# A three-layer network on one core: eight groups of four feature tiles as Strassen products

## The chip, the cores and the metric

The kernel runs on one NeuronCore of a Trainium2 chip. The metric is the device time of one launch in microseconds, median of several runs. 128-row tiles lie in on-chip memory (SBUF), matrix products accumulate in eight PSUM banks of 128x512 fp32. Five engines work side by side: TensorE (PE; PEld is its weight load), VectorE (DVE), ScalarE (ACT), GpSimd (POOL) and SyncE (SP), which issues most of the DMAs.

## What is computed

The reference takes `x` (512 tokens, 1024 features, fp32) through three layers: (a) a block with gated linear attention (GLA), dilated windowed attention, sigmoid gates over both, an MLP and an embedding gate; (b) an mLSTM with stick-breaking attention; (c) a multi-scale pooling layer. Only the start of the first layer matters here:

```python
h = rmsnorm(x, ln1[i])
hq, hk, hv, hr, ha, hatt, hgate = _split_cols(h @ w_in[i], SPLIT_SIZES)
# hatt: q, k, v of 3 groups x 4 heads x 128;  hq, hk, hv, hr: GLA;  hgate: two gates of 1024
g_gla, g_att = jnp.split(hgate, 2, axis=-1)
mix = (jax.nn.sigmoid(g_gla) * y_gla + jax.nn.sigmoid(g_att) * y_att) @ w_out[i]
```

So `h @ w_in` is a 512x1024 by 1024x9744 product in fp32 accuracy, whose columns feed attention, GLA and gates.

## The kernel before, in words

**Layout and accuracy.** Activations lie feature-major: eight tiles of 128 features by 512 tokens. Each fp32 operand is split into a rounded high part and a rest (`split`, L169: a copy on ScalarE into type fp32r, then a subtraction on VectorE). A product is three matmuls: high-high, high-low, low-high (`mm3`, L450; `mm`, L163).

**Chunks and units.** All weights are one stream, `wstream`, of 314 chunks of 128x1024 fp32 (512 KB), in the order of use. A unit of the program consumes one chunk. `fm` (L331) makes one output tile of 128 features by 512 tokens: 8 k-blocks by 3 matmuls of 512 columns, 24 in all. `tok` (L412) makes token-major tiles over several units. `fm(..., halves)` does the columns in two halves of 256, in a few places of layers two and three. PSUM gives four banks ("mm") to units and four ("q") to everything else.

**Order.** `run` (L285) walks the list of units. Before a unit it calls `split_chunk` (L214), which splits chunks up to three units ahead into one of four pairs of buffers (HL_BUFS) and issues DMAs of raw chunks (RAW_BUFS = 3). It then calls `pump` (L273), which advances up to two side generators (attention L878, GLA L1002) by a step when enough slots (units) have passed (LAG, L63) and PSUM banks are free, and takes one entry of `self.jobs`. Then it emits the unit's matmuls and its evacuation. The compiler orders each engine's queue once, before the run: an instruction earlier in this program order goes first, but one that is ready may overtake one that is not. On the chip every queue is then worked off in its order. All other tiles of 128x512 are taken from three pools of slots, 44, 16 and 16 (L51, `S` L96).

**Layer one.** `prologue` (L557) loads `xT` into `self.xt` and splits `ln1 * x`, not yet divided by the root mean square, into `xs` (16 tiles). `norm1` (L581) makes the factor per token, `r1`, in both layouts. Every evacuation of the layer then multiplies by it: `qk_unit` (L596) on VectorE (with a stride of four tokens for groups 1 and 2, "z order"), `v_units` (L610) on ScalarE, the gates (L674) by a multiplication on VectorE and a sigmoid on ScalarE. The units run thus: 6 q/k tiles of attention head 0, 12 of the three v products, then 18 q/k tiles of heads 1 to 3 (`qk_head1`, L625), each head followed by the start of its attention; the unit for GLA's decay (`narrow`, L356), 8 for GLA's v, then for each of four GLA heads q, k and two `sr` tiles; 8 gate tiles, a wait for all generators, and `yg`, `ya` (L685, L692) with the last 8 gate tiles between them.

## Time and profile before

| | us |
|---|---|
| median of 3 runs (range) | 1927.49 (1927.16 to 1927.97) |
| the profiled execution's own time | 1926.77 |
| its span, first to last instruction | 1925.1 |
| TensorE busy | 1902.5 |
| VectorE, ScalarE, GpSimd busy | 1090.1, 873.3, 93.7 |
| mean granted TensorE clock | 0.995 |
| HBM traffic | 178.55 MB read, 6.12 MB written, 96 GB/s |

The profile is of one execution; times in it count from its first instruction. Matmuls are pipelined: a matmul's own duration holds its way through the array, so the rate is read from a run of many of them, not from the duration of one. "Idle before" is the time for which the engine had nothing to do just before such an instruction, with what ended most of it. Instructions are named by the line of the helper that records them, so groups are told apart by shape and stretch. The profile finds a unit's end in the start of the ScalarE copy of the chunk four further on, which waits for that unit's buffer: by it 121.4 to 235 us holds the 18 q/k units of heads 1 to 3, 296.4 to 470 us the GLA heads and the first eight gates, 470 to 586 us `yg`, `ya` and the other eight gates.

### The profile page before, as it was taken

The numbers are of one execution on the slowest core, as the hardware profiler recorded it, in microseconds if no ns is written. First come the engines' busy times: TensorE is split into PE (matmuls) and PEld (weight loads), VectorE is DVE, ScalarE is ACT, GpSimd is POOL, SyncE is SP. The second block draws the span as 40 slices with busy tenths as digits, with TensorE's granted clock in tenths as the row PEclk, the third lists the DMA queues.
The fourth block names the chain that finished last, engine by engine and source line by source line (L and its number), as shares of the span: only waits on it lengthen the run. The fifth ranks groups of instructions, "written<-read, shape, count | busy, mean of one in ns | idle before, by whom it ended". The sixth has DMA issues, their size and how long they took to land.

```text
span 1925.1 us, 22678 instructions
## 1 busy us (share of the span) xinstructions
PE 1902.5 (99%) x8894; PEld 1598.1 (83%) x8894; DVE 1090.1 (57%) x1623; ACT 873.3 (45%) x1274; POOL 93.7 (5%) x125
## 2 busy tenths in 40 slices
PE   8999999999999999999998999999999999999998
PEld 7898888888888888888887888888888888888887
DVE  5245544577446543444556768677866627666733
ACT  4243344464223431333356666767666534433322
POOL 0000000000002000000120000011100011000000
PEclk9999999999999999999999999999999999999999
DMA  5442322222342322322232322222222322222222
GB/s 183 125 102 85 92 78 88 77 66 88 99 142 88 107 91 99 112 99 99 93 113 79 122 76 96 69 88 77 88 88 69 129 99 68 97 91 96 99 98 77
DMA packets 68095, 184.32 MB, mean 96 GB/s; under 512 B 17058, under 2 KB 20815, under 8 KB 67988
## 3 DMA queue, kind: packets, MB, share of 16 engines
q1 hardware_dynamic: 67412, 181.82, 29.3%
q8 instruction: 70, 1.15, 0.2%
q10 hardware_dynamic: 576, 1.05, 0.1%
q14 instruction: 37, 0.30, 0.0%
HBM read 178.55 MB, written 6.12 MB: 96 GB/s over the span
## 4 chain that ended last, share of the span: by engine, by line
PE 95%; DVE 3%; ACT 1%; issue 0%; DMA 0%; SPq 0%; POOL 0%; DVEq 0%; ACTq 0%; POOLq 0%
PE t L163 94%; DVE t L142 2%; ACT t L125 1%; DVE t L154 1%; PE t L973 0%; DMA t<-wstream 0%; PE t L1536 0%; ACT L125 0%; POOL t L500 0%; PE t L1045 0%; SPq L536 0%; ACT L136 0%; DVE t L1260 0%; SPq L533 0%; DVEq L1626 0%
## 5 line engine op out<-in xcount | busy, mean ns | idle before, releaser
L163 PE MATMUL t<-t,t 128*128 128x512 f32 (+3 forms) x8532 | 1862.2, 380 | 15.2 <-ACT t L125 9.4
L163 PEld LDWEIGHTS t<-t,t 128*128 128x128 f32 x8532 | 1549.9, 192 | 313.2 <-ACT t L125 12.7
L142 DVE TENSOR_TENSOR t<-t,t 128x1024 fp32r<-128x1024 f32 (+9 forms) x982 | 772.7, 815 | 718.4 <-ACT t L125 404.8
L125 ACT ACTIVATE t<-t 128x1024 fp32r<-128x1024 f32 (+6 forms) x883 | 633.8, 758 | 916.3 <-PE t L163 559.6
L154 DVE SCALAR_TENSOR_TENSOR t<-t,ct,t 128x512 f32<-128x512 f32 (+5 forms) x128 | 102.5, 815 | 15.4 <-ACT t L125 12.2
L154 DVE SCALAR_TENSOR_TENSOR t<-t,t 128x512 f32<-128x512 f32 (+6 forms) x112 | 76.4, 701 | 55.7 <-PE t L163 46.0
L125 ACT ACT_TABLE_LOAD x69 | 88.5, 1283 | 11.2 <-DVE t L154 8.6
L500 POOL TENSOR_TENSOR t<-t,t 128x512 f32<-128x512 f32 x33 | 52.2, 1588 | 577.0 <-ACT t L125 576.7
L125 ACT ACTIVATE t<-t,t 128x128 f32<-128x128 f32 (+4 forms) x93 | 50.3, 546 | 61.4 <-PE t L163 35.1
L125 ACT ACTIVATE t<-t,ct 128x512 f32<-128x512 f32 (+5 forms) x89 | 54.7, 624 | 19.9 <-DVE t L142 12.4
L197 POOL TENSOR_SCALAR_AFFINE_SELECT t<-t 128x128 f32<-128x128 f32 x80 | 36.4, 469 | 418.3 <-ACT t L125 222.4
L142 DVE TENSOR_TENSOR t<-t 128x511 f32<-128x511 f32 (+5 forms) x64 | 37.3, 586 | 1.2
L474 DVE RECIPROCAL t<-t 128x512 f32<-128x512 f32 (+3 forms) x15 | 28.1, 1870 | 13.6 <-ACT t L125 13.5
L154 DVE SCALAR_TENSOR_TENSOR t<-t,t,t 128x512 fp32r<-128x512 f32 (+3 forms) x41 | 27.6, 682 | 12.9 <-ACT t L125 12.7
L163 PE MATMUL t<-t,ct 128*128 128x256 f32 (+4 forms) x142 | 28.4, 335 | 0.0
L163 PEld LDWEIGHTS t<-t,ct 128*128 128x128 f32 (+1 forms) x142 | 21.5, 185 | 3.5 <-issue 1.0
L163 PEld LDWEIGHTS t<-ct,t 128*128 128x128 f32 x112 | 16.7, 220 | 0.7
L131 ACT ACTIVATE t<-t 128x512 f32<-128x512 f32 (+2 forms) x25 | 12.4, 561 | 10.3 <-PE t L163 7.7
L133 ACT ACT_TABLE_LOAD x13 | 16.7, 1283 | 0.2
L163 PE MATMUL t<-ct,t 128*128 128x1 f32 (+1 forms) x112 | 16.3, 278 | 0.0
L136 ACT ACTIVATE t<-t 128x512 f32<-128x512 f32 (+2 forms) x29 | 15.8, 594 | 0.2
L1517 ACT ACTIVATE t<-t 128x512 f32<-128x512 f32 x8 | 4.8, 598 | 23.7 <-PE t L163 23.7
(54 smaller groups left out, 133.0 us busy)
## 6 DMA issues: line engine op xcount, KB each, us to landing
t<-wstream SPq DMA_DIRECT2D x314, 512.0 KB, 3.3
t<-xT SPq DMA_DIRECT2D x16, 256.0 KB, 5.8
xdram<-t SPq DMA_DIRECT2D x8, 256.0 KB
t<-udram SPq DMA_DIRECT2D x8, 256.0 KB
t<-xdram SPq DMA_DIRECT2D x8, 256.0 KB, 5.5
out<-t ACTq DMA_DIRECT2D x4, 256.0 KB, 2.0
out<-t SPq DMA_DIRECT2D x4, 256.0 KB
skew<-bdram SPq DMA_DIRECT2D x2, 510.0 KB
```

The source lines that it names most:

```text
L125: self.pinned(self.nc.scalar.activation(out, in_, func, **kw))
L131: last = self.nc.scalar.activation(o, x, AF.Abs, bias=bias)
L133: last = self.nc.scalar.preload_act_table_set(EXPLN)
L136: last = self.nc.scalar.activation(o, o, AF.Exp, scale=-1.0)
L142: self.pinned(self.nc.vector.tensor_tensor(out, a, b, op=op))
L154: self.pinned(self.nc.vector.scalar_tensor_tensor(out, a, s, b, op0=op0, op1=op1))
L163: self.nc.tensor.matmul(out, lhsT, rhs, start=start, stop=stop, skip_group_check=True)
L197: self.nc.gpsimd.affine_select(t[:, 0:n], t[:, 0:n], pattern=[[1, n]], compare_op=op, fill=0.0, base=base, channel_multiplier=-1)
L474: self.nc.vector.reciprocal(out, out)
L500: self.nc.gpsimd.tensor_tensor(st[key], st[key], sq, op=ALU.add)
L1517: last = nc.scalar.activation(sq, ps, AF.Square, accum_out=ss[j][:, c:c + 1])
```

## The change

**Seven products for eight.** `quad` takes four feature tiles as two pairs. Each pair is a product of 256 features by 1024 by 512 tokens, seen as 2x2 blocks: two feature tiles, two halves of the features of `h`, two halves of the tokens. It is done in seven block products (Strassen's scheme in Winograd's form), each of 4 k-blocks by 3 matmuls of 256 columns. The seven units of a quad do the same product for both pairs, 24 matmuls of 256 columns each. Their weights come from four chunks, as before ("11", "12", "21", "22"); `third` makes the four sums of weight blocks on VectorE, and each of the seven blocks is split. The accumulators of a pair are two banks; the common partial sums are read out between the products (`snap`, ScalarE), and `c1` and `c2` put the output tiles together on VectorE and ScalarE. **Which groups:** 16 of the 18 q/k tiles of heads 1 to 3 (four quads), the q, k and `sr` tiles of GLA heads 0 and 1 (two) and the last eight gate tiles (two).

**Early normalisation.** Four jobs after `norm1` (`renorm`) multiply `xt` in place by `ln1` and `r1`, split the result into `xn` and build the sums of activation blocks (`forms`, `xf`). All units from the second v product on read `xn` or `xf`, and evacuate without `r1`, on ScalarE alone where VectorE multiplied before. `xs` ends after the first v product.

**Buffers.** One pool of 70 slots takes the place of 44, 16 and 16; RAW_BUFS goes from 3 to 6, of which three stay spare (one after the first layer's v products); `make` lets a unit take no chunk or two.

```diff
--- before.py
+++ after.py
 
-SLOTS = {'e': 44, 's': 16, 'r': 16}
-KIND = {"attention": "s", "gla": "r", "stick": "s", "mlstm": "r", "ml_out": "r", "ml_gates": "r"}
+SLOTS = 70
 TAIL = 2
...
+RAW_BUFS, HL_BUFS = 6, 4
+FAST_GLA, FAST_GATES = (0, 1), (4, 6)
 BIASW = (383, 255, 255)
 N_ONEHOT = sum(BIASW)
 
...
+
+    def raw_tile(self):
+        self.live += 1
+        return self.sb.tile([P, 1024], F32, name=self._nm(), tag="raw", bufs=RAW_BUFS)
+
+    def load_chunks(self, n=0):
+        while self.nd < self.nchunks and (self.nd < n or n == 0 and self.live < RAW_BUFS - self.spare):
...
             self.nc.sync.dma_start(t, self.io["wstream"][self.nd])
             self.raw[self.nd] = t
             self.nd += 1
 
+    def next_raw(self):
+        self.load_chunks(self.nr + 1)
+        self.nr += 1
+        return self.raw.pop(self.nr - 1)
+
+    def split_raw(self, raw):
+        h = self.sb.tile([P, 1024], F32R, name=self._nm(), tag="wh", bufs=HL_BUFS)
+        l = self.sb.tile([P, 1024], F32R, name=self._nm(), tag="wl", bufs=HL_BUFS)
+        self.act(h, raw, AF.Copy)
+        self.sub(l, raw, h.bitcast(F32))
+        return h, l
...
-            self.load_chunk(self.ns)
-            raw = self.raw.pop(self.ns)
-            h = self.sb.tile([P, 1024], F32R, name=self._nm(), tag="wh", bufs=HL_BUFS)
-            l = self.sb.tile([P, 1024], F32R, name=self._nm(), tag="wl", bufs=HL_BUFS)
-            self.act(h, raw, AF.Copy)
-            self.sub(l, raw, h.bitcast(F32))
-            self.hl[self.ns] = (h, l)
+            make = self.units[self.ns]["make"]
+            if make is None:
+                self.hl[self.ns] = self.split_raw(self.next_raw())
+                self.live -= 1
+            else:
+                self.hl[self.ns] = make()
             self.ns += 1
-            self.load_chunk(self.ns - 1 + RAW_BUFS)
+            self.load_chunks()
 
...
             return out
 
-        def both(out, r):
+        def both(out, r=None):
             n = out.shape[0]
+            if r is None:
+                self.act(out, st["ps"][0:n, :], AF.Copy)
+                self.add(out, st["ps"][64:64 + n, :], out)
+                return
...
+    def quad(self, specs, xf):
+        pairs = specs[0:2], specs[2:4]
+        st = [{} for _ in pairs]
+        r = {}
+
+        def take(*names):
+            for n in names:
+                r[n] = self.next_raw()
+
+        def done(n):
+            self.live -= 1
+            return self.split_raw(r.pop(n))
+
+        def first():
+            take("11")
+            return self.split_raw(r["11"])
+
+        def second():
+            take("12")
+            return self.split_raw(r["12"])
+
+        def third():
+            take("21", "22")
+            r["s1"] = self.raw_tile()
+            self.add(r["s1"], r["21"], r["22"])
+            self.sub(r["21"], r["11"], r["21"])
+            self.sub(r["11"], r["s1"], r["11"])
+            self.sub(r["12"], r["12"], r["11"])
+            return done("11")
+
+        makes = [first, second, third, lambda: done("s1"), lambda: done("21"), lambda: done("12"),
+                 lambda: done("22")]
+        L, R = HALVES
+
+        def order(t, z, sl=None):
+            if not z:
+                return t if sl is None else t[:, sl]
+            t = t.rearrange("p (z i) -> p z i", z=4)
+            return t if sl is None else t[:, :, sl.start // 4:sl.stop // 4]
+
+        def src(t, z):
+            return zs(t) if z else t
+
+        def compact(t, z):
+            return t.rearrange("p (z i) -> p z i", z=4) if z else t
+
+        def snap(p, bank, half, key, to, z, scale):
+            d = st[p]
+            if key not in d:
+                d[key] = self.S()
+            o = order(d[key], z, to) if key == "c1" else compact(d[key][:, to], z)
+            self.act(o, src(d[bank][:, half], z), AF.Copy, scale=scale)
+
+        def c1(p):
+            d = st[p]
+            _, _, _, func, scale, z, fin = pairs[p][0]
+            t = self.S()
+            self.stt(order(t, z), src(d["B"], z), scale, order(d["c1"], z), ALU.mult, ALU.add)
+            d["t1"] = t
+
+        def c2(p):
+            d = st[p]
+            t, t1 = self.S(), d["t1"]
+            _, _, _, func, scale, z, fin = pairs[p][1]
+            if pairs[p][0][3] is not None:
+                self.act(t1, t1, pairs[p][0][3])
+            self.act(order(t, z, L), src(d["A"][:, L], z), func or AF.Copy, scale=scale)
+            self.add(order(t, z, R), compact(d["c2"][:, L], z), compact(d["c2"][:, R], z))
+            if func is not None:
+                self.act(order(t, z, R), order(t, z, R), func)
+            pairs[p][0][6](t1)
+            fin(t)
+
+
+        steps = [("A", L, "11", True), ("B", L, "21", True), ("A", L, "t2", False), ("B", R, "t1", False),
+                 ("A", L, "t3", False), ("B", R, "22", False), ("A", L, "t4", False)]
+
+        def mk(i):
+            bank, half, form, fresh = steps[i]
+
+            def emit(h, l):
+                out = []
+                for p in range(2):
+                    d = st[p]
+                    if fresh:
+                        d[bank] = self.MM()
+                    ps = d[bank][:, half]
+                    fs = []
+                    for k in range(4):
+                        w = slice(p * T + k * P, p * T + (k + 1) * P)
+                        fs.append(lambda ps=ps, a=(h[:, w], l[:, w]), k=k: (
+                            self.mm3(ps, a, xf[form][k], fresh and k == 0, i > 2 and k == 3)))
+                    za, sa = pairs[p][0][5], pairs[p][0][4]
+                    zb, sb = pairs[p][1][5], pairs[p][1][4]
+                    if i == 0:
+                        fs.append(lambda p=p, z=za, s=sa: snap(p, "A", L, "c1", L, z, s))
+                    elif i == 2:
+                        fs.append(lambda p=p, z=za, s=sa: snap(p, "A", L, "c1", R, z, s))
+                    elif i == 3:
+                        fs.append(lambda p=p, z=zb, s=sb: snap(p, "B", R, "c2", L, z, s))
+                    elif i == 4:
+                        fs.append(lambda p=p, z=zb, s=sb: snap(p, "A", L, "c2", R, z, s))
+                    elif i == 5:
+                        fs.append(lambda p=p: c1(p))
+                    elif i == 6:
+                        fs.append(lambda p=p: c2(p))
+                    out.append(fs)
+                return out
+            return emit
+
+        def block(n, k0):
+            return [(q[n][0], q[n][1], (k0 + k) * P, q[n][2], P) for q in pairs for k in range(4)]
+        raws = [[block(0, 0)], [block(0, 4)], [block(1, 0), block(1, 4)], [], [], [], []]
+        for i in range(7):
+            self.group(self.unit(None, mk(i)) | {"blocks": raws[i], "make": makes[i]}, joint=0)
+
+
+    def forms(self, a, b, xf):
+        L, R = HALVES
+        u, v = self.S(), self.S()
+        self.sub(u[:, L], a[:, R], a[:, L])
+        self.sub(u[:, R], b[:, R], u[:, L])
+        self.sub(v[:, L], b[:, R], a[:, R])
+        self.sub(v[:, R], b[:, L], u[:, R])
+        for t, lo, hi in ((u, "t1", "t2"), (v, "t3", "t4")):
+            pair = self.split(t)
+            xf.setdefault(lo, []).append(self.cols(pair, 0, T // 2))
+            xf.setdefault(hi, []).append(self.cols(pair, T // 2, T // 2))
 
...
             self.rsq(self.rtok, ps[:, 0:8], D)
             self.r1 = self.spread(self.rtok)
+            self.jobs.extend(lambda k=k: renorm(k) for k in range(4))
+
+
+        xn, xf = [None] * KT, {}
+
+        def renorm(k):
+            for j in (k, k + 4):
+                t = self.xt[j]
+                self.stt(t, t, self.vec("ln1", j), self.r1)
+                xn[j] = self.split(t)
+            self.forms(self.xt[k], self.xt[k + 4], xf)
+            for key, j, sl in (("11", k, HALVES[0]), ("21", k + 4, HALVES[0]), ("22", k + 4, HALVES[1])):
+                xf.setdefault(key, []).append(tuple(t[:, sl] for t in xn[j]))
+            self.xt[k] = self.xt[k + 4] = None
         xs = self.xs
 
...
-                o = 4 if g else 0
-                self.act(VT[g][j], ps, AF.Copy, scale=self.rtok[:, o + j:o + j + 1])
-            self.tok([("w_in", 0, A_ATT + g * 1536 + 1024, T)], xs, g > 0, evac)
+                if g:
+                    self.act(VT[g][j], ps, AF.Copy)
+                else:
+                    self.act(VT[g][j], ps, AF.Copy, scale=self.rtok[:, j:j + 1])
+            self.tok([("w_in", 0, A_ATT + g * 1536 + 1024, T)], xn if g else xs, g > 0, evac)
 
...
+            return ("w_in", 0, col, None, P ** -0.5 if which == "q" else 1.0, g > 0,
+                    lambda t: AT[h][which].__setitem__(g, t))
+
+        def put(to, i):
+            return lambda t: to.__setitem__(i, t)
 
         self.oatt = [None] * 4
...
-        qk_head1(1)
-        self.go(self.attention(1, AT, VT))
-        qk_head1(2)
-        self.go(self.attention(2, AT, VT))
-        qk_head1(3)
+
+        def clear():
+            xs[:] = [None] * KT
+            self.spare = 1
+        self.do(clear)
+        qk = [qk_spec(h, g, w) for h in (1, 2, 3) for g in range(3) for w in "qk"]
+        for i in range(0, 16, 4):
+            self.quad(qk[i:i + 4], xf)
+            if i in (4, 8):
+                self.go(self.attention(i // 4, AT, VT))
+        for _, _, col, _, scale, z, fin in qk[16:]:
+            def evac(ps, scale=scale, fin=fin):
+                t = self.S()
+                self.act(t.rearrange("p (z i) -> p z i", z=4), zs(ps), AF.Copy, scale=scale)
+                fin(t)
...
-            for d in range(2):
-                def evac(ps, n=2 * h + d):
-                    G["sr"][n] = self.silu_psum(ps, self.r1)
-                self.group(self.fm("w_in", 0, A_R + (2 * h + d) * P, xs, evac))
-            self.go(self.gla(h, G))
-
...
+
+        def several(specs, fast):
+            if fast:
+                self.quad(specs, xf)
+            else:
+                for sp in specs:
+                    single(sp)
+
+        for h in range(4):
+            several([("w_in", 0, base + h * P, None, 1.0, False, put(G[nm], h))
+                     for nm, base in (("q", A_Q), ("k", A_K))]
+                    + [("w_in", 0, A_R + n * P, AF.Silu, 1.0, False, put(G["sr"], n))
+                       for n in (2 * h, 2 * h + 1)], h in FAST_GLA)
+            self.go(self.gla(h, G))
+
+
+        sg = {}
+
+        def gates(n0):
+            several([("w_in", 0, A_GATE + w * D + n * P, AF.Sigmoid, 1.0, False, put(sg, (w, n)))
+                     for n in (n0, n0 + 1) for w in range(2)], n0 in FAST_GATES)
 
         mix = [None] * 8
...
         self.wait()
         for n0 in (0, 2, 4, 6):
             if n0 >= 4:
-                for n in (n0, n0 + 1):
-                    gate(0, n)
-                    gate(1, n)
+                gates(n0)
             yg(n0)
             yg(n0 + 1)
             ya(n0)
 
 
```

In the rest of the file `S(kind=...)` and `split(x, kind)` lose their kind, and `blocks` becomes a list of chunks.

## Rows read from the trace of the kernel before

**Rows 1.** Page of the profile: busy time, granted clock in 40 slices, chain by engine.
```profile
PE 1902.5 (99%) x8894; PEld 1598.1 (83%) x8894; DVE 1090.1 (57%) x1623; ACT 873.3 (45%) x1274; POOL 93.7 (5%) x125
...
PEclk9999999999999999999999999999999999999999
...
PE 95%; DVE 3%; ACT 1%; issue 0%; DMA 0%; SPq 0%; POOL 0%; DVEq 0%; ACTq 0%; POOLq 0%
```

**Rows 2.** Timeline of TensorE, two unbroken runs: start us, us, instructions.
```profile
704.68 20.56 PE L163 MATMUL t<-t,t 128*128 128x512 f32 x90
...
1606.60 5.32 PE L163 MATMUL t<-t,t 128*128 128x256 f32 x43
```

**Rows 3.** Groups by shape, whole span or Rows 2's second run: busy us, mean ns, idle before.
```profile
L163 PE MATMUL t<-t,t 128*128 128x512 f32 x7480 | 1728.3, 391 | 8.2 <-ACT t L125 5.5 <-DVE t L142 2.5 <-DVE t L154 0.2
L163 PE MATMUL t<-t,t 128*128 128x256 f32 x43 | 5.3, 283 | 0.0
L142 DVE TENSOR_TENSOR t<-t,t 128x1024 fp32r<-128x1024 f32 x314 | 385.3, 1228 | 330.7 <-ACT t L125 328.3 <-POOL t L500 0.8
L125 ACT ACTIVATE t<-t 128x1024 fp32r<-128x1024 f32 x314 | 331.6, 1059 | 731.9 <-PE t L163 538.9 <-issue 176.6 <-DMA t<-wstream 13.8
L142 DVE TENSOR_TENSOR t<-t,t 128x512 f32<-128x512 f32 x306 | 216.2, 716 | 299.8 <-PE t L163 254.8 <-ACT t L125 23.1 <-ACT t L1517 18.6
L142 DVE TENSOR_TENSOR t<-t,t 128x512 fp32r<-128x512 f32 x179 | 123.0, 692 | 46.3 <-ACT t L125 42.8
L154 DVE SCALAR_TENSOR_TENSOR t<-t,ct,t 128x512 f32<-128x512 f32 x40 | 29.1, 750 | 2.8 <-PE t L163 2.7
L142 DVE TENSOR_TENSOR t<-t,t 128x256 f32<-128x256 f32 x58 | 25.5, 473 | 1.6 <-PE t L163 1.4
L125 ACT ACTIVATE t<-t 128x256 f32<-128x256 f32 x6 | 2.4, 395 | 4.2 <-PE t L163 3.9 <-DVE t L142 0.3
```

**Rows 4.** Busy time by stretch (us): PE, PEld, DVE, ACT, POOL, granted clock, DMA.
```profile
121.40:235.00 113.60, 113.60 (x567) 96.23 (x566) 59.23 (x160) 35.25 (x84) 1.08 (x2) 1.00 0.29 88
296.40:470.00 173.60, 173.60 (x833) 143.22 (x832) 113.19 (x139) 92.00 (x122) 0.53 (x1) 1.00 0.24 79
470.00:586.00 116.00, 116.00 (x513) 96.04 (x513) 59.74 (x68) 36.93 (x45) 3.55 (x2) 1.00 0.37 120
```

**Rows 5.** Groups of VectorE by shape in 121.4 to 235 us.
```profile
L142 DVE TENSOR_TENSOR t<-t,t 128x1024 fp32r<-128x1024 f32 x19 | 23.1, 1219 | 1.6 <-ACT t L125 1.6
L142 DVE TENSOR_TENSOR t<-t,t 128x512 f32<-128x512 f32 x10 | 9.7, 972 | 16.0 <-PE t L163 16.0
L154 DVE SCALAR_TENSOR_TENSOR t<-t,t 128x512 f32<-128x512 f32 x9 | 8.5, 942 | 16.4 <-PE t L163 16.4
```

**Rows 6.** Waits of VectorE in 121.4 to 235 us: total, times, longest.
```profile
DVE t L142 <- DMA t<-t: 13.2, 3, 7.8
...
DVE t L932 <- ACT t L125: 3.3, 2, 1.6
```

**Rows 7.** Busy time in two early stretches, columns as in Rows 4.
```profile
36.90:63.10 26.20, 26.20 (x114) 20.37 (x113) 10.27 (x10) 5.31 (x5) 0.00 (x0) 1.00 0.29 91
63.10:82.00 18.90, 18.90 (x83) 17.50 (x82) 1.23 (x1) 3.82 (x5) 0.00 (x0) 1.00 0.50 145
```

**Rows 8.** Timeline of VectorE, 28 to 64 us: two evacuations of the first tiles.
```profile
34.60 0.69 DVE L154 SCALAR_TENSOR_TENSOR t<-t,t 128x512 f32<-128x512 f32 x1 [5.02 <-ACT t L125]
...
48.07 2.21 DVE L142 TENSOR_TENSOR t<-t,t 128x512 f32<-128x512 f32 x2 [3.23 <-PE t L163]
```

**Rows 9.** Timeline of ScalarE in one attention head: first and last of 12 exponentials.
```profile
165.22 0.40 ACT L125 ACTIVATE t<-t,t 128x128 f32<-128x128 f32 x1 [4.22 <-DVE t L158]
...
170.10 0.19 ACT L125 ACTIVATION_READ_ACCUMULATOR t<-t,t 128x1 f32 x1
```

**Rows 10.** Busy time around a wait of TensorE, columns as in Rows 4.
```profile
1018.00:1023.20 5.20, 1.50 (x6) 0.91 (x6) 4.75 (x10) 4.64 (x9) 0.00 (x0) 1.00 0.35 134
1023.30:1026.70 3.40, 3.40 (x16) 3.40 (x17) 2.51 (x7) 1.21 (x3) 0.00 (x0) 0.51 0.67 233
```

104 lines of the change are left out of this document (48 added, 56 removed).

## The prediction

> **What bounds the kernel now.** I read the page's busy times, clock and chain first. TensorE is busy 1902.5 of 1925.1 us at full clock in all 40 slices, and 95% of the chain that ends last is its own [rows 1]. So the time is the matmuls' spacing times their number, plus some 22.6 us of start, tail and waits. VectorE at 57% and ScalarE at 45% matter only where a stretch loads them far above that share. That asks for two more views: the timeline of unbroken matmul runs, for the spacing by width, and busy time by stretch, for the room beside TensorE in layer one.
>
> Spacing: 90 matmuls of 512 columns take 20.56 us [rows 2]; less the 0.39 us that the last one lasts [rows 3], over 89, that is 226.6 ns. 43 of 256 columns take 5.32 us [rows 2]; less 0.283 [rows 3], over 42, 119.9 ns. Half the columns cost 53% of the time, not half: some 13 ns go with each matmul whatever its width.
>
> **The change part by part.**
>
> *Matmuls (on the path).* A pair of tiles takes 2x24 matmuls of 512 columns, 48 x 226.6 ns = 10.88 us. After: 7 products x 4 k-blocks x 3 = 84 matmuls of 256 columns, 84 x 119.9 ns = 10.07 us. That is 0.805 us a pair; eight quads hold 16 pairs: **12.9 us less**. An eighth of the products goes, but the 13 ns per matmul take 40% of that back (16 x (10.88 - 84 x 113.3 ns) would be 21.8 us). The 256-column run shown has the same pattern (high twice, then low) with new weights each time, so I take its price unchanged.
>
> The Trainium skill, "TensorE: Matmul & The Clock Gate", section "Back-to-back issue gap", gives N/2.4 + 2.5 ns, so 215.8 and 109.2 ns; by it the saving would be 16 x (48 x 215.8 - 84 x 109.2) ns = 19.0 us. The rows are 5% and 10% above it, so the trace does not agree, and its 12.9 us stands.
>
> *VectorE and ScalarE in a quad (beside the matmuls, if they fit).* Before, four units need 4 x (1.22 split + 0.96 evacuation) = 8.7 us of VectorE [rows 5] in 4 x 24 x 0.2266 = 21.8 us. After, a quad lasts 2 x 10.07 = 20.1 us and needs 7 splits and 4 sums of 128x1024, 11 x 1.22 = 13.4 us, two `c1` at about 0.95 [rows 5], two half-width adds at 0.47 [rows 3]: **16.2 us of 20.1**. The fp32 sum of 128x1024 isn't in the trace; between the split's 1.23 and two 512-column operations, 1.43 [rows 3], I take the split's (same width). ScalarE: 7 x 1.06 + 10 half reads x 0.40 [rows 3] = 11.4 us, up to some 2.5 more with Silu or sigmoid. Should z-ordered half reads take twice that, ScalarE has 15.4 of 20.1. So alone, a quad fits, and lookahead helps: splits run three units, 3 x 2.88 = 8.6 us, ahead, and copy plus split take 2.3, which leaves VectorE 6.3 us to be late before TensorE feels it.
>
> *Quads beside attention.* In 121.4 to 235 us VectorE is busy 59.2 us [rows 4]; less splits and evacuations, 41.3 [rows 5], 17.9 us belong to some 2.2 attention heads, 8 each. In-order waits add 13.2 for DMA and 3.3 for ScalarE [rows 6], 7.5 a head, in which nothing behind can run. Matmuls beside the units: 113.6 - 18 x 5.44 = 15.7 us [rows 4], some 5.2 a head as counted for three. The stretch after: TensorE 113.6 - 6.4 (eight pairs) = 107.2; VectorE 17.9 + 4 x 16.2 + 2 x 1.2 = 85.1, with waits 101.6. It still fits, but not evenly: quads one and two share head 0 (VectorE 32.4 + 15.5 = 47.9 against TensorE 40.2 + 5.2 = 45.4: 2.5 behind, inside the lookahead); quads three and four each have nearly a head of their own, 31.7 against 25.3, 6.4 behind. The third uses up the lookahead (0.1 over), the fourth has none left: up to 6.4 us of waiting, **0 to 6.5** in all, zero if splits are queued into the waits. ScalarE adds one thing: a head's 12 exponentials hold it 165.22 to 170.29, 5.1 us [rows 9], and the next product into a half bank that `snap` reads comes 3 half units, 4.3 us, later; 5.1 + 0.4 - 4.3 = 1.2 us a head, **0 to 3.6** for three. Bounds 0 and 10.1; heads are ordered with priority over what comes later, yet the compiler has slack to fill, so I take the middle, **5.0 us**.
>
> *Quads in GLA and gates.* 296.4 to 470 us: VectorE 113.2 of 173.6 [rows 4]. Two quads add 2 x 7.5; the 16 single tiles lose one multiplication of 0.72 [rows 3] each to ScalarE, which has 92.0 busy there. So 117 of 170. Only the second quad has a generator (GLA head 0) beside it: 113.2 less 26 splits (31.7) and 24 evacuations (17.2) is 64.3, 16 a head, some 10 of it in a quad's seven slots: 26.2 against 20.1 and some 2 of GLA's matmuls, 4.1 behind, inside 6.3. In 470 to 586 VectorE has 59.7 of 116.0 [rows 4]; two quads add 15. I take **0** for both; without the lookahead 4.1.
>
> *Early normalisation.* VectorE: 8 scalings x 0.75, 16 splits x 0.69, 16 half-width subtractions x 0.47 [rows 3] = 24.5 us; ScalarE 16 copies, 10 us. `r1` stands at 34.6 us [rows 8]; VectorE is busy 10.3 of 26.2 us to 63.1 and 1.2 of 18.9 after [rows 7]: 33.6 us free before the second v product is well under way, ScalarE has more. It costs **0**, covered by the first v product's 12 us of idle VectorE. The wait it adds: evacuations of the q/k tiles stand behind earlier jobs. The last one, at 48.1 us [rows 8], comes some 8 later, and the first v product wants four banks at once from 48 on. TensorE can use the other banks first, if so queued; 0 to **8 us**, I take 0.
>
> *DMAs.* The chunks stay 314, four per quad. `third` needs two at once, loaded five deep rather than three, so 0; behind a late one on SP's queue stand only later chunks. *One pool of 70 for 76, raw buffers 3 to 6.* No row shows a wait for a slot as such. Idle TensorE is 22.6 us in all [rows 1]: it could give back a few of them or add as many; I take 0 and 3 us either way. The v evacuations stay on ScalarE: nothing.
>
> **Sum.** -12.9 + 5.0 = -7.9 us. On the profiled execution: 1926.8 - 7.9 = 1918.9; the median stands 0.7 above that execution (its span is 1.7 below its time), so **1919.6 us**, which is 0.4% less. A measurement of this kernel can tell about 0.2%, 3.9 us, from no change.
>
> **Rivals.**
>
> *All of it is hidden (0.25).* The compiler fills VectorE's waits with splits, and nothing is given back: 1927.5 - 12.9 = 1914.6. For: VectorE's sum, 101.6 with every wait, is below TensorE's 107.2. Against: bursts of attention, and queues fixed before the run.
>
> *The waits take it all (0.18).* Attention's upper bound, 10.1, plus GLA's 4.1, less what lookahead saves in one of them: the result lies within 3.9 us of 1927.5. For: VectorE at 80% of a quad before any attention.
>
> *VectorE becomes the bound: slower (0.17).* Wherever a generator or the early jobs stand in front of a unit's split or evacuation, TensorE waits for VectorE's queue: 10.1 in attention, 8 at the first v product, 4.1 in GLA, 22.2 in all. It decides from 12.9 us of waits on; then 1927.5 - 12.9 + 22.2 = 1936.8. For: the in-order waits on DMA [rows 6] happen wherever the units are short. Against: TensorE has no such wait there today.
>
> *The clock falls with the waits (0.06).* After 5.20 us in which TensorE ran 1.50, the next 3.40 us ran at a granted clock of 0.51, the 1.2 GHz level: 16 matmuls of 256 columns [rows 10] where 28 would have gone, 1.4 us lost. If the 5.0 us above came in two or three such waits, 3 to 4 more: 1923. It needs waits of several us together, which my budget has only in quad four. The Trainium skill says the same in "TensorE: Matmul & The Clock Gate", "HAM oscillation — how this bites in real kernels": gaps between bursts of matmuls throttle the clock again. By that rule the time is this rival's, not the forecast's; the trace agrees that it happens.
>
> *Matmuls at the page's gap (0.01).* 19.0 rather than 12.9 saved, 1913.5; rows 2 speak against it.
>
> **How the numbers follow.** The forecast, waits of 2 to 8 us, has 0.33 and its own range 1916 to 1922. Faster by over 0.2% (under 1923.6): 0.33 + 0.25 + 0.01 + half of 0.06 = 0.62. Within 0.2%: 0.18 + 0.03 = 0.21. Slower: 0.17. The range runs from 1913.5, full hiding with 1 us of drift elsewhere, to 1932.0; that leaves out most of the slower case and little else.
>
> **What would show it.** Right: 84 matmuls at 120 ns per pair, so 1344 more of 256 columns and 768 fewer of 512; the split of the chunk after the last attention tile some 6 us less the waits earlier; VectorE above 75% in 121 to 230 us; TensorE's new waits few, on VectorE's subtraction or ScalarE's copy, in quads three and four. Wrong: 256-column matmuls above 120 ns in the quads; gaps near 48 to 60 us (early jobs); gaps in quads one and two, or in the gates; a granted clock under 1 in layer one after 50 us; new waits in layers two and three (the pool).

## The result, and the profile after

The changed kernel takes **1961.5 us** (median of 4 runs, 1959.9 to 1962.4) against 1927.3 for the kernel before beside it: ratio 1.0177, interval 1.016 to 1.0195. It is slower by 34 us where 8 less were forecast. The profiled execution has a span of 1960.3 us, 35.2 more than before.

The page of the changed kernel: busy time, granted clock in 40 slices, chain by engine and by line, answering to [rows 1].

```profile
PE 1904.2 (97%) x9470; PEld 1621.7 (83%) x9470; DVE 1151.3 (59%) x1699; ACT 922.3 (47%) x1394; POOL 92.2 (5%) x125
...
PEclk9999999999999999999999999999999999999999
...
PE 85%; DVE 7%; ACT 4%; issue 2%; DMA 2%; SPq 0%; POOL 0%; DVEq 0%; ACTq 0%; POOLq 0%
PE t L163 84%; DVE t L142 5%; ACT t L125 2%; DVE t L154 1%; DMA t<-t 1%; ACT L125 1%; PE t L1163 1%; DVE t L1508 0%; DMA t<-wstream 0%; POOL t L197 0%; DVE t L1082 0%; ACT t L136 0%; DMA t<-skew 0%; ACT L133 0%; PE t L1726 0%
```

TensorE fills 85% of the chain, not 95%; VectorE went from 3 to 7%. Busy TensorE is no shorter, though an eighth of the products in the quads is gone: part of its time runs at a lower clock. The page hides that (in each slice of 49 us the clock still shows as 9, which is 90% or more); the stretches show it.

Groups of TensorE by shape in the changed kernel (busy us, mean ns, idle before):

```profile
L163 PE MATMUL t<-t,t 128*128 128x512 f32 x6712 | 1562.6, 392 | 21.2 <-DVE t L142 10.8 <-ACT t L125 6.1 <-DVE t L154 4.3
L163 PE MATMUL t<-t,t 128*128 128x256 f32 x1952 | 257.4, 289 | 11.8 <-ACT t L125 6.6 <-DVE t L154 4.0 <-DVE t L142 1.0
...
L1163 PE MATMUL t<-ct,t 128*128 128x128 f32 x60 | 12.3, 348 | 8.1 <-DVE t L158 8.1
```

The matmuls of 512 columns are 768 fewer, as counted. The waits in front of them grew from 8.2 us [rows 3] to 21.2, and the transposes of attention (L1163) got 8.1 of their own.

Busy time by stretch of the changed kernel, columns as in [rows 4]: first the five stretches of layer one's projections, then three of layers two and three.

```profile
36.90:121.40 84.50, 83.44 (x368) 75.45 (x367) 39.12 (x57) 28.74 (x41) 0.00 (x0) 1.00 0.29 90
121.40:235.00 113.60, 102.30 (x796) 99.95 (x795) 78.79 (x202) 64.62 (x157) 0.00 (x0) 0.95 0.27 80
235.00:296.40 61.40, 57.06 (x289) 48.30 (x288) 32.85 (x100) 25.36 (x57) 0.74 (x1) 0.97 0.33 99
296.40:470.00 173.60, 173.09 (x1005) 150.95 (x1004) 106.05 (x123) 100.38 (x145) 1.05 (x2) 1.00 0.26 85
470.00:586.00 116.00, 116.00 (x671) 102.89 (x670) 80.16 (x93) 54.57 (x80) 0.00 (x0) 1.00 0.34 114
...
1010.00:1130.00 120.00, 110.50 (x562) 93.78 (x561) 79.21 (x113) 69.29 (x101) 16.77 (x18) 0.97 0.30 101
1280.00:1420.00 140.00, 132.35 (x611) 109.53 (x610) 98.82 (x135) 87.20 (x128) 10.94 (x25) 0.98 0.22 72
1420.00:1560.00 140.00, 134.88 (x618) 111.67 (x618) 92.39 (x123) 85.50 (x123) 9.16 (x20) 0.99 0.25 80
```

The last three stretches of the kernel before:

```profile
1010.00:1130.00 120.00, 114.82 (x589) 98.22 (x588) 79.78 (x122) 81.34 (x116) 9.25 (x18) 0.99 0.29 95
1280.00:1420.00 140.00, 140.00 (x659) 117.37 (x658) 94.14 (x129) 94.46 (x135) 11.58 (x23) 1.00 0.26 86
1420.00:1560.00 140.00, 137.47 (x639) 115.28 (x638) 88.06 (x114) 79.32 (x109) 11.87 (x17) 1.00 0.29 98
```

There are two losses, in two places. In 36.9 to 586 us TensorE idles 549.1 - 531.9 = 17.2 us, where the rows of before show none [rows 4, 7], and the clock of 0.95 and 0.97 costs some 7 us more: some 24 lost against 12.9 saved, **some 11 us net**. In the last three stretches, where the changed kernel computes nothing differently, it idles 22.3 us against 7.7 and runs at 0.97 to 0.99: some 21 us.

**A mark for every run.** To place a loss I take the start of the 164th weight split from the end (ScalarE's 128x1024 copies, 892.3 us in the kernel before, in layer one's MLP). Its shift is the loss *up to the mark*; the shift of the span less that is the loss *behind it*. With three or five buffers of split weights in place of four, splits stand one chunk, 24 x 0.2266 = 5.4 us, later or earlier against the matmuls; that is taken off (the last split shows the same 5.4 to 5.5 against the span).

| kernel | slot pools | up to the mark | behind it | median us | ratio to before |
|---|---|---|---|---|---|
| after | one | +12.5 | +22.7 | 1961.5 | 1.0177 |
| pool70, pool76 | one | +7.2, +5.7 | +27.5, +24.8 | 1957.2, 1957.1 | 1.0164, 1.0161 |
| singles | one | +5.1 | +28.3 | 1954.5 | 1.0153 |
| lag | one | +0.5 | +24.1 | 1949.9 | 1.0122 |
| singles_lag | one | 0.0 | +22.9 | 1951.3 | 1.0119 |
| lag_snap | one | +8.4 | +25.6 | 1961.1 | 1.0168 |
| late_quads | one | -5.2 | +26.9 | 1944.8 | 1.0100 |
| pool72_hl5 | one | +6.2 | +22.1 | 1954.2 | 1.0151 |
| lag_hl3 | one | +16.2 | +28.6 | 1971.9 | 1.0236 |
| two_60_16 | two | +0.9 | -3.7 | 1923.9 | 0.9977 |
| two_60r16 | two | +5.2 | -2.8 | 1931.5 | 1.0020 |
| after_s12 | two | +18.8 | +4.4 | 1952.0 | 1.0134 |
| lag_s12 | two | +15.4 | +5.9 | 1949.4 | 1.0118 |
| gates_only_s12 | two | +13.6 | +6.6 | 1946.5 | 1.0104 |
| lag_r5_s12 | two | +8.4 | -2.7 | 1930.9 | 1.0014 |
| gates_lag_s12 | two | +11.1 | -4.2 | 1933.4 | 1.0029 |
| **late_quads_s12** | two | -4.5 | -2.3 | **1920.0** | **0.9961** |

Both columns of losses are read from one execution of each kernel. pool70 and pool76 are the same instructions in the same order (below) and differ by 1.5 and 2.7 us in them, so differences of that size say nothing. The kernel before took 1924.6 to 1927.9 us beside these kernels, so between rows compare ratios rather than medians.

### The profile page after: what moved, and what is told of

It is laid out like the page before. It is cut to its first block, busy times and chain, and to the rows that moved or that the text cites. A ratio compares the mean times of both kernels' runs of the same rounds, so it can differ in the third digit from the quotient of the medians.

```text
span 1960.3 us, 24052 instructions
## 1 busy us (share of the span) xinstructions
PE 1904.2 (97%) x9470; PEld 1621.7 (83%) x9470; DVE 1151.3 (59%) x1699; ACT 922.3 (47%) x1394; POOL 92.2 (5%) x125
## 4 chain that ended last, share of the span: by engine, by line
PE 85%; DVE 7%; ACT 4%; issue 2%; DMA 2%; SPq 0%; POOL 0%; DVEq 0%; ACTq 0%; POOLq 0%
PE t L163 84%; DVE t L142 5%; ACT t L125 2%; DVE t L154 1%; DMA t<-t 1%; ACT L125 1%; PE t L1163 1%; DVE t L1508 0%; DMA t<-wstream 0%; POOL t L197 0%; DVE t L1082 0%; ACT t L136 0%; DMA t<-skew 0%; ACT L133 0%; PE t L1726 0%
## 5 line engine op out<-in xcount | busy, mean ns | idle before, releaser
L163 PE MATMUL t<-t,t 128*128 128x512 f32 (+2 forms) x9108 | 1863.4, 366 | 34.2 <-DVE t L142 13.0
L163 PEld LDWEIGHTS t<-t,t 128*128 128x128 f32 x9108 | 1572.5, 193 | 306.8 <-DVE t L142 17.1
L142 DVE TENSOR_TENSOR t<-t,t 128x1024 fp32r<-128x1024 f32 (+8 forms) x1023 | 820.2, 832 | 679.2 <-ACT t L125 464.2
L125 ACT ACTIVATE t<-t 128x1024 fp32r<-128x1024 f32 (+6 forms) x1026 | 700.9, 728 | 929.7 <-PE t L163 552.6
L154 DVE SCALAR_TENSOR_TENSOR t<-t,t 128x512 f32<-128x512 f32 (+6 forms) x119 | 78.8, 680 | 65.3 <-ACT t L125 51.7
L154 DVE SCALAR_TENSOR_TENSOR t<-t,ct,t 128x512 f32<-128x512 f32 (+5 forms) x136 | 107.3, 810 | 13.6 <-ACT t L125 9.2
L125 ACT ACTIVATE t<-t,t 128x128 f32<-128x128 f32 (+4 forms) x77 | 39.0, 515 | 31.0 <-PE t L163 12.2
L142 DVE TENSOR_TENSOR t<-t 128x256 f32<-128x256 f32 (+5 forms) x84 | 45.7, 550 | 1.4
L154 DVE SCALAR_TENSOR_TENSOR t<-t,t,t 128x512 fp32r<-128x512 f32 (+3 forms) x41 | 27.3, 682 | 17.2 <-ACT t L125 13.2
L1163 PE MATMUL t<-ct,t 128*128 128x128 f32 x60 | 12.3, 348 | 8.1 <-DVE t L158 8.1
L1163 PEld LDWEIGHTS t<-ct,t 128*128 128x128 f32 x60 | 9.6, 177 | 9.8 <-DVE t L158 8.9
L131 ACT ACTIVATE t<-t 128x512 f32<-128x512 f32 (+2 forms) x25 | 12.5, 559 | 8.1 <-PE t L163 8.1
L163 PEld LDWEIGHTS t<-ct,t 128*128 128x128 f32 x112 | 15.7, 208 | 0.6
```

The lines of the kernel that those rows point to most:

```text
L125: self.pinned(self.nc.scalar.activation(out, in_, func, **kw))
L131: last = self.nc.scalar.activation(o, x, AF.Abs, bias=bias)
L142: self.pinned(self.nc.vector.tensor_tensor(out, a, b, op=op))
L154: self.pinned(self.nc.vector.scalar_tensor_tensor(out, a, s, b, op0=op0, op1=op1))
L163: self.nc.tensor.matmul(out, lhsT, rhs, start=start, stop=stop, skip_group_check=True)
L1163: nc.tensor.transpose(ps[:, b * P:(b + 1) * P], L[t][:, b * P:(b + 1) * P], self.ident)
```

## The experiments

**One pool alone.** pool70 and pool76 are the kernel before with one pool, of 70 slots here and of 76:

```diff
-SLOTS = {'e': 44, 's': 16, 'r': 16}
+SLOTS = 70
-        k = kind or self.kind
-        return self.sb.tile([p, n], dt, name=self._nm(), tag=k, bufs=SLOTS[k])
+        return self.sb.tile([p, n], dt, name=self._nm(), tag="s", bufs=SLOTS)
```

Expected of pool70: 

> The kernel before with one pool of 70 slots in place of 44, 16 and 16, nothing else changed. Theory A (the one pool is what costs layers two and three some 22.7 us): about 1950 us, with new waits of TensorE between 1030 and 1520 us of the span as in the changed kernel, layer one as before. Rival (the losses of layers two and three come with the quads, the early normalisation or the raw buffers): 1927 us, within 0.2%.

Expected of pool76: 

> The same with one pool of 76, so that only the partition goes and no slot is lost. If the number of slots is the cause (70 for 76): about 1927 us. If having one pool is the cause, because work that is ready early takes slots that the units need: about 1945 to 1950 us, near the run with 70.

Both lose some 31 us with no block product in them: 1.0164 (1.0141 to 1.0186) and 1.0161 (1.014 to 1.0182). It isn't the number of slots: 70 and 76 give the same instruction lists, in the same order, on TensorE, VectorE and ScalarE. What differs from before is the order: set side by side with that of before, the list of TensorE's last 4,600 instructions differs in some 400 lines in pool76 and in some 20 in two_60_16 (below). The count alone does not tell a bad order from a harmless one: two_60r16 (below) differs in some 250 and loses nothing behind the mark.

Up to the mark the loss is one wait of TensorE, at 155 us, for attention's transposes (total, times, longest; pool76, 121 to 250 us), and the lower clock behind it:

```profile
PE t L971 <- DVE t L157: 3.0, 1, 3.0
```

**Two pools.** two_60_16 joins `e` and `r` (60) and leaves attention's and stick-breaking's `s` apart (16); two_60r16 joins `e` and `s` and leaves `r` apart. The edit of the first:

```diff
-SLOTS = {'e': 44, 's': 16, 'r': 16}
+SLOTS = {'e': 60, 's': 16}
         k = kind or self.kind
+        k = 'e' if k == 'r' else k
```

> The kernel before with two pools: 60 slots for the units, GLA and mLSTM, 16 for attention and stick-breaking. If it is attention and stick-breaking running ahead that costs time when they are not held to 16 slots: about 1927 to 1932 us. If it is mLSTM and GLA: about 1950 us, with the waits at 1057 to 1520 us as in pool76 and none at 152 us.

> The kernel before with two pools the other way: 60 slots for the units, attention and stick-breaking, 16 for GLA and mLSTM. If attention and stick-breaking run ahead when not held to 16 slots: about 1950 us or more, with the wait at 152 us of pool76. If mLSTM and GLA do: about 1932 us, with the wait at 152 us alone.

With either kind apart the loss behind the mark is gone: 0.9977 (0.9968 to 0.9987), a little faster than before, and 1.002 (1.001 to 1.003). Each time fits what was expected if one kind is to blame, but the two runs blame opposite kinds: so neither kind alone makes that loss, it takes all three in one pool. two_60r16 keeps 5.2 us up to the mark, with a wait of 5.0 us at the transposes; two_60_16 has none there. What TensorE waits for in 1010 to 1560 us (total, times, longest), in pool76:

```profile
PE t L162 <- DVE t L141: 12.3, 7, 3.9
PE t L1270 <- DVE t L141: 6.0, 1, 6.0
PE t L162 <- ACT t L124: 2.9, 4, 1.4
PE t L162 <- DVE t L153: 2.3, 3, 1.0
```

and in two_60_16 (each line number two or three higher):

```profile
PE t L164 <- ACT t L126: 2.8, 4, 0.9
PE t L1273 <- DVE t L143: 1.2, 1, 1.2
PE t L164 <- DVE t L155: 0.9, 2, 0.5
PE t L164 <- DVE t L143: 0.6, 1, 0.6
```

The difference is the wait for VectorE's tensor-tensor operations, 18.3 us against 1.8. One such wait in pool76, VectorE's timeline and then TensorE's:

```profile
1386.33 3.35 DVE L1316 RECIPROCAL t<-t 128x512 f32<-128x512 f32 x1
1389.59 2.95 DVE L141 TENSOR_TENSOR t<-t,t 128x512 fp32r<-128x512 f32 x4
```

```profile
1384.73 2.22 PE L162 MATMUL t<-t,t 128*128 128x512 f32 x12 [0.64 <-DVE t L153]
1390.87 11.33 PE L162 MATMUL t<-t,t 128*128 128x512 f32 x44 [3.92 <-DVE t L141]
```

The operation on a 512-column tile that TensorE's next matmuls wait for stands behind a reciprocal of 3.35 us in VectorE's queue. That is no lack of VectorE (95.9 us busy of the 140 from 1280); it is what stands ahead of what. The same wait comes again at 1518 us, and one of 6.0 us stands at 1064 us. All ten kernels with one pool have the two waits of 3.9 to 4.1 us, and nine of them the one of 6.0; none of the eight with two pools has any of the three. Only the wait shown here was followed to what stands ahead of it.

**A fifth buffer of split weights.** The edit against pool76:

```diff
-SLOTS = 76
+SLOTS = 72
-RAW_BUFS, HL_BUFS = 3, 4
+RAW_BUFS, HL_BUFS = 3, 5
```

> The kernel before with one pool of 72 slots and five buffers of split weights instead of four. Theory: what the single pool costs in layers two and three is TensorE waiting for VectorE's remainder subtraction of weights that stand behind other work in its queue; a fifth buffer lets that subtraction be queued one chunk earlier and mends most of it: 1930 to 1942 us. Rival (the loss is in the order of the generators' own steps, which the number of weight buffers doesn't touch): 1950 us or more, as with four buffers (1957).

1954.2 us, 1.0151 (1.0135 to 1.0166): the rival holds. The same lines, 12.3 and 6.0 us, stand in the list of waits, and none of their eight waits ends with the subtraction of a weight split (128x1024): all are for tiles of at most 512 columns. So it is the generators' steps among each other that come in a worse order, not weight splits that start too late.

**The block products, with one pool.** singles computes all 32 tiles of the quads as single tiles and keeps the early normalisation (attention's heads 1 and 2 then start behind six and twelve tiles, as before, not behind eight and twelve); lag doubles the slots between attention's steps; singles_lag does both; lag_snap moves lag's half-bank reads to VectorE.

```diff
singles, singles_lag:
-        for i in range(0, 16, 4):
-            self.quad(qk[i:i + 4], xf)
+        for i, (_, _, col, _, scale, z, fin) in enumerate(qk):
...
+            self.group(self.fm("w_in", 0, col, xn, evac))
-FAST_GLA, FAST_GATES = (0, 1), (4, 6)
+FAST_GLA, FAST_GATES = (), ()
lag, singles_lag, lag_snap:
-LAG = {'attention': (2, 5, 2), ...
+LAG = {'attention': (2, 10, 4), ...
lag_snap:
-            self.act(o, src(d[bank][:, half], z), AF.Copy, scale=scale)
+            self.ts(o, src(d[bank][:, half], z), scale, ALU.mult)
```

singles: 

> The changed kernel with every quad turned into single tiles: early normalisation, one pool and six raw buffers stay. Theory A with the quads blamed for layer one alone: layer one within 3 us of the kernel before (no waits of 17.8 us, full clock, but also no saving of 12.9), layers two and three still some 22.7 us longer, so about 1950 us. Rival (early normalisation costs layer one): layer one 5 us or more longer than before at its end, 1955 us or more. Rival (the quads upset the later layers): 1927 to 1931 us.

lag: 

> The changed kernel with the attention generators' steps ten and four slots apart instead of five and two. Theory B (a slot of a quad lasts 2.9 us instead of 5.4, so attention's transposes stand in TensorE's queue before VectorE has scaled their inputs): the 8.1 us of TensorE waiting at the transposes go, and some of the 7 us lost to the lower clock, so layer one ends 8 to 13 us earlier and the total is 1948 to 1954 us. Rival (VectorE's sums and splits of the quads hold TensorE): layer one unchanged, 1961 us.

singles_lag: 

> No quads (every tile single, as in the run singles), attention's steps ten and four slots apart. It splits what the longer spacing gave into what it gives to the quads and what it gives to the one pool. If the spacing mends only the quads: as singles, about 1954 us. If attention's transposes also wait without quads, because one pool lets the compiler queue attention early (one wait of 2.5 us at 152.9 us and a lower clock behind it in singles): layer one 4 to 6 us shorter, about 1949 us, and then the quads are worth nothing in the run lag.

lag_snap: 

> The run lag with the half-bank reads of a quad (snap) on VectorE in place of ScalarE. Theory C (TensorE's wait of 3.6 us at 138 us is a half-bank read queued behind attention's 12 exponentials on ScalarE; that of 3.2 us at 196.6 us is one queued behind an exponential that waits, by way of VectorE, for a DMA): the wait at 138 us goes, 3.6 us and 1.5 to 4 us of lower clock; the one at 196.6 stays, since VectorE waits for the same DMA; 1943 to 1946 us. Rival (VectorE is the scarcer engine in a quad): its queue grows by 64 half reads of 0.4 us, and TensorE waits as long or longer, 1950 to 1960 us.

singles takes 1954.5 us, with 5.1 up to the mark. By that number its rival, that the early normalisation costs layer one 5 us, would hold; but pool70 and pool76 lose 7.2 and 5.7 there without it. lag takes 1949.9 us and theory B holds: layer one is 12.0 us shorter than in the changed kernel. singles_lag, 1951.3 us, lies between its two figures, and up to the mark it is 5.1 us shorter than singles, as the second has it. lag_snap, 1961.1 us, loses the wait at 138 us as theory C said, but misses its time by 15 us and lies above the range of its rival too.

Up to the mark singles_lag stands where the kernel before does (0.0): the early normalisation costs nothing that the mark can show. Against singles the quads cost 7.4 us with the old spacing (after), and against singles_lag 0.5 with the new one (lag). The two spacings differ because `LAG` counts slots, and a slot of a quad lasts 24 x 119.9 ns = 2.9 us where a single tile's lasts 5.4. Not all that the longer spacing gave is the quads': it took 5.1 us off without any.

What TensorE waits for in 121 to 250 us, in the changed kernel:

```profile
PE t L1163 <- DVE t L158: 8.1, 3, 3.7
PE t L163 <- ACT t L125: 4.4, 3, 3.5
PE t L163 <- DVE t L154: 3.1, 2, 2.4
```

The first line is attention's transposes. VectorE's timeline around one such wait, and TensorE's:

```profile
149.66 2.94 DVE L142 TENSOR_TENSOR t<-t,t 128x8 f32<-128x8 f32 x8 [3.20 <-DMA t<-t]
...
153.30 0.80 DVE L158 TENSOR_SCALAR t<-t,t 128x128 f32<-128x128 f32 x3
```

```profile
149.83 0.76 PE L163 MATMUL t<-t,t 128*128 128x256 f32 x5
153.63 2.24 PE L1163 MATMUL t<-ct,t 128*128 128x128 f32 x12 [3.04 <-DVE t L158]
```

The head's row sums go through memory; VectorE waits 3.20 us for them, scales, and only then can TensorE transpose. The transposes stand in TensorE's own queue ahead of the next products. With ten slots this line is gone (lag has none up to 586 us). Three waits make the 8.1 us; pool76 and singles, without any quad, have one of them, 3.0 and 2.3 us at 155 us, so the first, shown here, can be the pool's as well as the quads'. The second line stays: the read of a half bank stands behind the head's 12 exponentials on ScalarE, which end at 141.2, and they in turn stand behind a copy of weights and the load of a table. ScalarE's timeline (the exponentials cut out; the read is the second of the last five instructions), then TensorE's:

```profile
133.82 1.06 ACT L125 ACTIVATE t<-t 128x1024 fp32r<-128x1024 f32 x1 [0.69 <-PE t L163]
134.90 1.28 ACT L125 ACT_TABLE_LOAD   x1
...
141.16 1.94 ACT L125 ACTIVATE t<-t 128x8 f32<-128x8 f32 x5
```

```profile
141.67 6.53 PE L163 MATMUL t<-t,t 128*128 128x256 f32 x40 [3.45 <-ACT t L125]
```

The 6 us right behind that wait and behind the three others of over 2 us, columns as in [rows 4], have a granted clock of 0.72, a mixture of the 1.2 and 2.4 GHz levels. That is 1.7 us lost behind each, 6.7 in all:

```profile
141.70:147.70 6.00, 6.00 (x38) 6.00 (x39) 3.09 (x4) 2.46 (x5) 0.00 (x0) 0.72 0.07 1
153.70:159.70 6.00, 6.00 (x36) 5.54 (x37) 4.03 (x14) 3.89 (x9) 0.00 (x0) 0.72 0.53 171
204.40:210.40 6.00, 4.69 (x27) 4.49 (x27) 6.00 (x21) 1.60 (x3) 0.00 (x0) 0.72 0.00 1
244.10:250.10 6.00, 6.00 (x27) 5.17 (x28) 2.19 (x11) 2.49 (x5) 0.00 (x0) 0.72 0.26 89
```

Two stretches of lag and of singles_lag tell where the 12.9 us went. lag:

```profile
121.40:200.00 78.60, 71.09 (x575) 70.07 (x573) 58.19 (x140) 45.81 (x110) 0.00 (x0) 0.97 0.30 88
200.00:296.40 96.40, 96.40 (x554) 85.83 (x555) 56.84 (x166) 44.31 (x105) 0.89 (x1) 0.97 0.31 86
```

singles_lag:

```profile
121.40:200.00 78.60, 78.60 (x375) 66.07 (x374) 35.19 (x144) 33.17 (x83) 0.00 (x0) 1.00 0.41 116
200.00:296.40 96.40, 96.40 (x497) 82.18 (x496) 37.47 (x117) 41.53 (x97) 0.61 (x1) 1.00 0.28 82
```

7.5 us of waits and 3% of 175 us, 5.2, by the clock: 12.7 of the 12.9 given back. lag_snap shows that ScalarE was still the better place for the reads: TensorE's waits move to VectorE (9.7 us on its L142 in 121 to 296 us) and it is 8 us worse up to the mark.

**Block products only where no attention runs.** late_quads is singles_lag with `FAST_GLA, FAST_GATES = (0, 1), (4, 6)` put back.

> The changed kernel with the longer spacing of attention, queries and keys as single tiles, and block products only for the groups of GLA heads 0 and 1 and of the gates 4 and 6: no attention runs beside a block product any more. Four quads save 8 x 0.8 = 6.4 us. Theory (block products pay where no exponentials stand ahead of their half-bank reads on ScalarE): 6 us below the 1951.3 of all single tiles, 1943 to 1947 us. Rival (they pay nowhere, since TensorE waits for their reads wherever they stand): 1950 to 1954 us.

The theory holds: 1944.8 us, and -5.2 up to the mark, of 8 x 0.805 = 6.4 saved; TensorE waits 1.6 us in 37 to 590 us. It is the mark that shows it: by the medians the kernel is 6.5 us under singles_lag, by the ratios 3.7, and their intervals overlap (1.0083 to 1.0118 against 1.0104 to 1.0134).

**Both repairs together.** The changed kernel's tiles leave no room for a second pool of 16, so the first four kernels of this kind have pools of 62 and 12 and three weight buffers; lag_hl3 is their control, one pool of 74.

```diff
-SLOTS = 70
+SLOTS = {'e': 62, 's': 12}
+KIND = {"attention": "s", "stick": "s"}
-RAW_BUFS, HL_BUFS = 6, 4
+RAW_BUFS, HL_BUFS = 6, 3
```

after_s12: 

> The changed kernel with the slots of attention and of the stick-breaking generator apart again (12 of them, 62 for everything else); to make room, three buffers of split weights instead of four. If one pool for all three kinds lets the compiler queue these generators too early (theory), the 22.7 us of layers two and three come back and most of the 5 to 7 us that the pool costs in layer one, and the quads' own waits stay: 1930 to 1940 us. If the loss of the later layers has another cause, or 12 slots and three weight buffers cost as much again (rival): 1955 us or more.

lag_s12: 

> The same two pools, with the longer spacing of attention (2, 10, 4). Theory: lag measured 1949.9 us, of which 24.6 us were lost after layer one; these come back, so 1922 to 1930 us. If the block products' 12.9 us also survive in layer one, 1915 us. Rival (another cause of the later loss): 1945 us or more.

gates_only_s12: 

> The same two pools; block products only for the two groups of gates, where no attention runs; all other groups as single tiles. Two quads save 4 x 0.8 = 3.2 us of TensorE. Theory (the loss sits in the pool and in the quads beside attention): 1919 to 1927 us. Rival (the early normalisation and the VectorE work that comes with it cost of themselves): 1932 us or more.

lag_hl3: 

> A control: the kernel with the longer spacing and one pool, with three weight buffers instead of four and 74 slots. Theory: the two sizes alone mend nothing, 1945 to 1956 us (lag measured 1949.9). Rival (what the two-pool kernels gain comes from splitting weights less far ahead, not from the pool): 1930 us or less.

By their times all four missed the theory, and the table says why: two things were changed. The third buffer's loss costs lag 15.7 us up to the mark (lag_hl3 against lag), which I had not expected; behind it, lag_s12 has 5.9 where lag_hl3 has 28.6: what the pool costs there came back.

The last three keep four weight buffers, and give up one of six raw buffers and two of 24 small tiles for pools of 61 and 12:

```diff
+SLOTS = {'e': 61, 's': 12}
+RAW_BUFS, HL_BUFS = 5, 4
-        return self.sb.tile([p, n], F32, name=self._nm(), tag="m", bufs=24)
+        return self.sb.tile([p, n], F32, name=self._nm(), tag="m", bufs=22)
```

late_quads_s12: 

> The kernel with block products only beside GLA and gates, with the slots of attention and stick-breaking apart (12, and 61 for the rest) and four buffers of split weights; the room comes from five raw weight buffers instead of six and 22 small tiles instead of 24. Theory (the pool's loss in layers two and three goes, the 5.2 us of the block products in layer one stay): 1944.8 less 17 to 23 us, 1922 to 1928 us. If five raw buffers cost nothing in layer one, 1920 us, faster than before. Rival (five raw buffers, all of them held by one group of four, stop the prefetch of weights beside it): 1935 us or more.

lag_r5_s12: 

> The whole change (block products beside attention too, longer spacing) with the same two pools and sizes. Theory: the block products beside attention are worth nothing or less (lag lost 12.5 us of 12.9 in waits and clock in layer one), so 3 to 7 us slower than late_quads_s12, 1926 to 1934 us. Rival (the pool, not the place, was what made them wait): faster than late_quads_s12, 1916 us.

gates_lag_s12: 

> The same with block products only for the gates 4 and 6. Theory: 3.2 us less saved than with the GLA groups, 1925 to 1931 us. Rival (the five raw buffers stop the prefetch beside a group of four): as fast as late_quads_s12 or faster, having half the groups.

late_quads_s12 takes **1920.0 us**, 0.9961 (0.9949 to 0.9974): it beats both kernels, and is where the theory put it if five raw buffers cost nothing. Its page:

```profile
PE 1897.1 (99%) x9182; PEld 1606.2 (84%) x9182; DVE 1112.4 (58%) x1655; ACT 909.2 (47%) x1360; POOL 101.9 (5%) x125
...
PE 90%; DVE 5%; ACT 2%; issue 1%; DMA 0%; SPq 0%; POOL 0%; DVEq 0%; ACTq 0%; POOLq 0%
```

Not all of that is the block products': two_60_16, without any, is at 0.9977. What can be theirs is the 4.5 us up to the mark.

With the products beside attention as well (lag_r5_s12) it is 1930.9, 1.0014 (1.0005 to 1.0023): inside its theory's range, and 10.8 slower than late_quads_s12 rather than 3 to 7. Not all of that is the place of the products: up to the mark it stands at +8.4 where lag, with one pool and six raw buffers, has +0.5, and TensorE idles 13.0 us in 121 to 296 us, lag 7.5. Which of the changed sizes does it was not tested.

gates_lag_s12 is slower than either bound of its theory, 1933.4, 1.0029 (1.0017 to 1.004): TensorE idles 6.8 us in 400 to 590 us, nearly all in two waits of 3.4 and 2.8 for ScalarE, at 421 and 458 us. That is ahead of its gate quads, which start at about 503 us:

```profile
400.00:500.00 100.00, 93.25 (x416) 75.53 (x415) 66.80 (x78) 55.76 (x75) 0.00 (x0) 0.93 0.15 53
500.00:590.00 90.00, 90.00 (x557) 81.42 (x556) 57.74 (x66) 41.73 (x63) 0.86 (x1) 1.00 0.41 141
```

The clock of 0.93 costs some 7 us more. Both waits fall among single tiles and end with a ScalarE activation that comes right behind the load of a table (1.28 us). gates_only_s12 has the same two, 2.9 us each at 424 and 460 us, so its miss is not the third buffer's alone. Of the 15.6 us between this kernel and late_quads_s12 up to the mark only 3.2 are the price of two quads fewer; the two waits and the clock behind them are about the rest. Why single tiles wait here, and not in singles_lag with its one pool, was not followed up.

## Why the prediction was wrong

**Failed: "One pool of 70 for 76 ... I take 0 and 3 us either way".** The pool costs 22 to 29 us behind the mark in every kernel with one pool, and some 5 to 7 before it at the old spacing. I read pools as capacity: "No row shows a wait for a slot as such". True, and beside the point. The pools go into the order in which the compiler lays out each engine's queue, and no view of the kernel before shows an order that it does not have. My bound, "idle TensorE is 22.6 us in all", limits what can be gained; for a loss it is no bound. The list of what would prove it wrong did name "new waits in layers two and three (the pool)"; the range did not hold it. Shown: one pool makes the loss, a second one removes it, and the number of slots, 70 or 76, doesn't matter. Open: by which rule one pool gives the worse order.

**Failed: "Quads beside attention", 0 to 10.1, taken at 5.0.** It measured 15.6 us of waits, one of which, of 3.0 us, may be the pool's, as pool76 has it without any quad; those at 141.7 and 153.6 us fall in quads one and two, which the step had as safe. The step set VectorE's work against a lookahead of weight splits, and ScalarE's exponentials at 1.2 us a head. It left out TensorE's own queue: attention's transposes (8.1 us) stand in it and wait for a chain through memory, whose distance `LAG` counts in slots that a quad halves. The price of a head's exponentials was too low: 3.45 us in one wait, not 1.2. The "3 half units later" held (the product into the half bank ended at 133.9 us, TensorE stopped at 138.2), but ahead of the 12 exponentials the read also had the copy of weights and the load of the table, 1.06 + 1.28 us; with the 1.2 that makes 3.5. Only one head of three paid it, so the bound of 3.6 for three held. VectorE's throughput was not the matter: 78.8 us busy in 113.6 [rows 4 have 59.2], against the 85.1 worked out. That working also dropped the 2.5 us that quads one and two were behind; carried on to the third, they make its bound 9.0 and not 6.5.

**Undersized: the clock.** I gave it 0.06 and 1.4 us a wait, because "my budget has only" one long wait. With four waits of 2.4 to 3.7 us in 121 to 250 us it cost 6.7 us in layer one, 1.7 each: the price of a wait was near, the number of waits was not. The mechanism was as read in [rows 10].

**Right.** Matmuls: 768 fewer of 512 columns, and those of 256 in the quads start 120 ns apart (median); the four late quads gave 5.2 of 6.4. Early normalisation: taken at 0, two early waits of 0.8 and 0.3 us at 53.1 and 59.3 us. GLA and gates: 0 in the changed kernel (0.5 us idle in 296 to 586). The sums of weight blocks: 1.22 us each. Of the rivals, "VectorE becomes the bound: slower" had the sign and not the cause: TensorE does wait for VectorE, more in layers that the change does not touch than in layer one, and VectorE was never full.

## What to carry to other kernels

A buffer pool is not only room: where a compiler orders the queues, merging or splitting pools moves instructions, and that is tested by itself, without the rest of a change, before anything is costed at zero. Spacings counted in units of work must be counted again when a unit gets shorter. Faster arithmetic on a bound engine pays only where nothing waits for another engine's queue: here 5.2 of 6.4 us beside GLA and gates, nearly nothing of 12.9 with attention among them. And a changed order alone can cost more than such arithmetic saves, as gates_lag_s12 shows.

## What the runs showed of the hardware

In the changed kernel the clock fell behind waits of 2.4 to 3.7 us, not only after a stretch of 5.2 us as in [rows 10]: 0.72 over the 6 us behind each of four. In lag it is 0.97 as the mean of 200 to 296.4 us, where TensorE has no idle time left, only the wait of 3.1 us that ended at 199.9 us before it. Not every wait has this price: behind one of 2.5 us in the kernel before, the clock stayed at 1.00:

```profile
1492.70:1498.70 6.00, 6.00 (x27) 4.96 (x28) 4.61 (x8) 4.25 (x6) 0.00 (x0) 1.00 0.05 20
```

So a wait can be paid again behind itself, in the changed kernel by 6.7 us for 15.6 in 121 to 250 us.
